# Moving adaLN accumulations, expert loads, key transposes and one shift vector within the hand-written order of an attention stage

## The chip, the cores and the metric

The kernel runs on one core of a Trainium2 chip. The metric is the device time of one execution in microseconds (us), median of three runs. TensorE (PE) multiplies and transposes, VectorE (DVE) and ScalarE (ACT) work on the results, GpSimd (POOL) takes some elementwise work, and SyncE (SP) issues nearly all transfers from the chip's memory, one after another in its own program order.

## The reference, cut to what matters

One layer of a diffusion transformer over 256 latent tokens `x` and 256 context tokens, width 1024, in float32:

```
mod = split(silu(c) @ w_ada + b_ada, 6)              # six vectors of 1024
h   = modulate(rms_norm(x), mod[0], mod[1])           # context tokens likewise, with c_ctx
y   = token_mixing(h, hc, ...)                        # 8 heads windowed GQA with sinks, 8 heads MLA, @ w_o
x   = x + mod[2] * rms_norm(y)
h2  = modulate(rms_norm(x), mod[3], mod[4])
f   = moe_ffn(h2, ...)                                # router, top 4 of 32 experts, clamped SwiGLU
x   = x + mod[5] * rms_norm(f)
```

The weights of the 32 experts are 32 x 12 MB. Every expert is computed, for the tokens that chose it, so all 384 MB are read in each execution.

## The kernel before, in words

The program has three stages: projections (to about 117 us), attention (to about 237 us) and experts (to the end).

**Attention.** The 16 heads are worked in 8 units of two heads, u = 0 to 3 for GQA and u = 4 to 7 for MLA. For each unit `weights(u)` computes the transposed logits on PE into PSUM tiles (named `mm`, four buffers shared by nearly everything in this stage) and takes their exponential on ACT; `adds(u)` sums them on POOL; `values(u)` multiplies by the values on PE and divides on DVE; `mix(u)` multiplies the unit's output by its part of `w_o` and adds into the four tiles `y`. A softmax needs a shift, the largest logit of a row: `top_a` and `top_b` compute it (PE, then a DVE reduce into `mx`), and `shift(g)` turns the sign on DVE, transposes on PE (L649) and copies to `nmax` on ACT (L651), which `weights` then adds by a matmul with `sel`. `shift("a")` serves units 0 to 3, `shift(0)` units 4 and 5, `shift(1)` units 6 and 7. For MLA the keys of four token blocks are prepared by `k_mid(i)` (two ACT copies, L529 and L530, the first of which reads the projection `pk[i]` out of PSUM) and `k_flip(i)` (eight PE transposes, L536, into two `tp` buffers; ACT casts, L137, with a DVE partner).

**Ada pieces.** Of the six adaLN vectors, four are accumulated along the way: index `ch` 0 (`mod[2]`, tile `accw_105`, called `vmix`), 1 (`mod[3]`, `accw_106`), 2 (`mod[4]`, `accw_107`), 3 (`mod[5]`, `vpost`). Each takes four loads of 1 MB of `w_ada`, so there are 16 pieces. `ada_load()` issues the DMA of the next piece (L418) into a tile of the three-buffer ring `slot`, or of a small pool `ax`; `ada_do()` takes the oldest loaded piece and adds it with two DVE instructions of 128x1024 (L431, called a pair here). `ada(1)` in the attention stage is a load of the next piece and the pair of an older one. When a vector's four pieces are in, `column(1)`, `column(2)`, `spread1(0)` and `spread1(3)` use it: a column is eight small matmuls and DVE work, `spread1` is two halves, each two PE instructions in the trace (L604) and one DVE product (L605). `router_bias()` needs `column(1)`.

**Expert loads.** `load(e, js)` issues 1 MB pieces of the expert weights, each into the next of 18 buffers in the order `RSEQ`; the three-buffer ring `slot` is among them, so an expert load there waits until the ada piece before it in that buffer has been consumed. The first three go out in the middle of attention, the others from `load(0, range(3, 6))` on. In the expert stage L1021 is the matmul with an expert's weights, and a later load waits until PE has finished with the buffer's former content.

**Order.** From L749 on the order on every engine, SP's queue included, is the order in which the code calls these functions; nothing is rearranged. Semaphores between engines are set from the data and the buffers. The calls are the list that starts with the two `ada_load()` behind `manual_schedule` and ends with `mix(KD - 1)`.

Of the kernel before, what the change touches and what calls it, by code (L numbers as in the profile page):

```python
# [70 lines left out]
def layer_kernel(ctx, tc, x, cx, cc, wadr, bada, grows, win0, winB, winC, winD, wuqa, wuqb, wukv, wo, wr, wexp, bgu, bgx, bdn, cols, rows, consts, out):  # L71
# [335 lines left out]
    ada_n = [0]  # L407
    ada_q = []
# [12 lines left out]
    def ada_do(n=1):  # L421
        for _ in range(n):
            ch, s, w = ada_q.pop(0)
            a = accs[ch]
            for k in range(2):
                sk = silu[:, 2 * s + k, 0:1]
                if (ch, s, k) in ADA_G:
                    S.activation(w[:, k], w[:, k], AF.Copy, scale=sk)
                    G.tensor_tensor(a, a, w[:, k], op=ALU.add)
                else:  # L430
                    V.scalar_tensor_tensor(a, w[:, k], sk, a, op0=ALU.mult, op1=ALU.add)  # L431
# [10 lines left out]
    def top_a(j, t):  # L442

        s_ = [pmm((P, 512)) for h in range(2)]
        kb = 3 - t
        for h in range(2):
            PE.matmul(s_[h][:, kb * P:(kb + 1) * P], ident_b, mask_b[:, t * P:(t + 1) * P], start=True, stop=False,
                      skip_group_check=True)
        for h in range(2):
            PE.matmul(s_[h], qTg[0][HALF[h], t, j], kTg[0][HALF[h]], start=False, stop=True, skip_group_check=True)  # L450
        for h in range(2):
            V.tensor_reduce(mxs["a"][:, t, 64 * h + j:64 * h + j + 1], s_[h], axis=AX.X, op=ALU.max)
# [35 lines left out]
    def up(i, p_, ws):  # L488
        for k in range(2):
            mm3(p_, (ckvT[0][:, i, k], ckvT[1][:, i, k]), ws[k], k == 0, k == 1)  # L490
        return p_

    for t in range(NT):
        top_a(3, t)
    ada_do()
    pk = {i: up(i, prow() if i < 2 else pmm(), ws) for i in (2, 3, 0, 1)}
    st1.close()
# [29 lines left out]
    def k_mid(i):  # L527
        k96[i] = pqa.tile([P, 8, 96], F32, name="k96", tag="ct", bufs=2)
        S.copy(k96[i][:, :, 0:64], pk[i].rearrange("p (h d) -> p h d", h=8))  # L529
        S.copy(k96[i][:, :, 64:96], krt[:, i][:, None].to_broadcast([P, 8, 32]))  # L530

    def k_flip(i):
        for g in range(2):
            pt = ptp((96, 4, P))
            for j in range(4):
                PE.transpose(pt[:, j], k96[i][:, g * 4 + j], ident)  # L536
            ks = slice(i * P, (i + 1) * P)
            split(kTm[0][g][0:96, :, ks], kTm[1][g][0:96, :, ks], pt)
# [57 lines left out]
        S.dma_start(gs_[ch], bass.AP(tensor=grows.tensor, offset=grows.offset + (0 if ch == 0 else 1) * D,  # L596
                                             ap=[[0, P], [1, D]]))

    def spread1(ch):
        a, gs = accs[ch], gs_[ch]  # L600
        for n in range(2):
            sl = slice(n * 512, (n + 1) * 512)
            p_ = pmm((P, 512))
            PE.matmul(p_, ones_f, a[:, sl], start=True, stop=True)  # L604
            V.tensor_tensor(a[:, sl], p_, gs[:, sl], op=ALU.mult)  # L605
# [25 lines left out]
    def top_b(h):  # L631
        n, j = divmod(h, 4)
        for t in range(NT):
            s_ = pmm((P, 512))
            PE.matmul(s_, qTm[n][0:96, 0, t, j], kTm[0][n][0:96, j], start=True, stop=True)
            V.tensor_reduce(mxs[n][:, t, j:j + 1], s_, axis=AX.X, op=ALU.max)

    def shift(g):

        m = mxs[g]  # L640
        if g == "a":
            m4 = m.rearrange("p t (h c) -> p t h c", h=2)[:, :, :, 0:4]
            V.scalar_tensor_tensor(m4, m4, -1.0, nsink.rearrange("p (h j) -> p h j", h=2)[:, None].to_broadcast([P, NT, 2, 4]),
                                   op0=ALU.mult, op1=ALU.min)
        else:
            V.tensor_scalar(m[:, :, 0:4], m[:, :, 0:4], -1.0, None, op0=ALU.mult)
        p_ = pmm((P, T))
        for t in range(NT):
            PE.transpose(p_[:, t * P:(t + 1) * P], m[:, t], ident)  # L649
        r = rows_[g] = av.tile([P, T], F32R, name="nmax", tag="nmax", bufs=2)  # L650
        S.copy(r, p_)  # L651
        if g == "a":
            for h in range(2):
                ess[h] = av.tile([P, T], F32, name=f"es{h}")
                S.activation(ess[h], r.bitcast(F32), AF.Exp, scale=A_SCALE, bias=col[:, G_SINK + h:G_SINK + h + 1])
# [4 lines left out]
    def weights(u):  # L660

        a = u < 4
        pT_[u] = [av.tile([P, 4, T], F32, name="pT", bufs=4) for h in range(2)]
        for g in range(2):
            st = [pmm((P, 2, T)) for h in range(2)]
            for kk in range(2):
                kt = 2 * g + kk
                ks = slice(kt * P, (kt + 1) * P)
                ops = []
                for h in range(2):  # L670
                    if a:
                        k_ = [x_[HALF[h], ks] for x_ in kTg]
                        q_ = [x_[HALF[h], :, u] for x_ in qTg]
                        sl, r = sel[HALF[h], u], rows_["a"][HALF[h]]
                    else:
                        n, j = divmod(2 * (u - 4) + h, 4)
                        k_ = [x_[n][0:96, j, ks] for x_ in kTm]
                        q_ = [qTm[n][0:96, i, :, j] for i in range(2)]
                        sl, r = sel[0:96, j], rows_[n][0:96]
                    ops.append([(k_[0], q_[0]), (k_[0], q_[1]), (k_[1], q_[0]), (sl, r)])  # L680
                for i in range(4):
                    for h in range(2):
                        PE.matmul(st[h][:, kk], *ops[h][i], start=(kk == 0 and i == 0), stop=(i == 3 and not (a and g)),  # L683
                                  skip_group_check=True)
                if a and g:
                    t = 3 - kt
                    for c in range(2):
                        for h in range(2):
                            PE.matmul(st[h][:, kk, t * P + c * 64:t * P + c * 64 + 64], mask_s[HALF[h], t, c],
                                      ident_b[HALF[h], HALF[h]], start=False, stop=True, skip_group_check=True)  # L690
            for h in range(2):
                S.activation(pT_[u][h][:, 2 * g:2 * g + 2], st[h], AF.Exp, scale=A_SCALE if a else B_SCALE)  # L692
        adds(u)
# [58 lines left out]
    ada_load()  # L752
    v_split()
    k_mid(2)
    k_mid(3)
    shift("a")
    weights(0)
    k_flip(2)
    k_mid(0)
    weights(1)  # L760
    k_flip(3)
    k_mid(1)
# [37 lines left out]
    shift(0)  # L800
    top_b(4)
    top_b(5)
    mix(2)
    column(1)
    weights(4)
    ada(1)
    top_b(6)
    top_b(7)
    mix(3)
    load_wo(3)  # L810
    ada(1)
    router_bias()
    spread1(0)
    shift(1)
    weights(5)
    ada(1)
# [2 lines left out]
    weights(6)  # L819
    mix(4)  # L820
    ada(1)
    column(2)
    values(5)
    spread0(3)
    ada(1)
    load(0, range(3, 6))
    weights(7)
    mix(5)
    ada(1)
    values(6)  # L830
    load(0, range(6, 8))
    load(1, range(0, 1))
    ada(1)
    mix(6)
    assert ada_n[0] == 16 and not ada_q
    values(7)
    spread1(3)
    mix(KD - 1)
    st2.close()
    stB.close()  # L840
# [515 lines left out]
```

## Time and profile before

| what | value |
|---|---|
| runs | 1195.87, 1200.46, 1198.42 us; median 1198.42 us |
| profiled execution | 1200.95 us, span of its trace 1199.2 us |
| PE busy | 1106.7 us, 92% of the span |
| DVE, ACT, POOL busy | 304.8, 231.4, 129.2 us |
| mean granted clock of TensorE | 0.980 |
| data moved | 446.58 MB, 372 GB/s over the span |

The span is the time from the first to the last instruction of the profiled execution; its run time is 1.75 us longer. The granted clock is told as a share of full speed: 1.00 is 2.4 GHz, 0.50 is 1.2 GHz. In the rows below, a mark such as [2.17 <-ACT nmax L651] behind an instruction says that its engine was idle for 2.17 us ahead of it and that this ended with ACT's writing of `nmax` at line 651. A row of a timeline may hold several instructions of one kind (x4); its second number is the time from the first one's start to the last one's end.

### The profile page before, as it was taken

The page shows a single profiled execution, that of the slowest core. Times are in us where ns is not written, and L with a number is a line of the kernel's source. Part 1 is how long each engine was busy: PE and PEld are TensorE (multiplying, and loading weights), DVE is VectorE, ACT ScalarE, POOL GpSimd, SP SyncE. Part 2 cuts the span into 40 slices and gives each one's busy share as a digit, 9 for nine tenths or more (in the row PEclk, how much of TensorE's full clock was granted, in tenths as well). Part 3 has the DMA queues.
Part 4 walks back from the last instruction along what each step waited for, and adds up shares of the span by engine and source line. Part 5 has one row for each costly group of instructions (what it writes and reads, how often), then busy time and mean ns, then how long its engine had stood idle before and what let it go on. Part 6 is the DMA issues. An engine that isn't in the chain of part 4 may idle for free.

```text
span 1199.2 us, 13600 instructions
## 1 busy us (share of the span) xinstructions
PE 1106.7 (92%) x5441; PEld 475.2 (40%) x5441; DVE 304.8 (25%) x651; ACT 231.4 (19%) x509; POOL 129.2 (11%) x186
## 2 busy tenths in 40 slices
PE   7699999999999999999989999999899999999985
PEld 2587757553343434333333333333333333333321
DVE  3776566742111111111111111111111111111112
ACT  3533612121111111111111111111111111111101
POOL 0301413210101010100101010101010101010000
PEclk9889999998999999999999999999999999999998
DMA  9740093899999999999999999999999999999994
GB/s 379 300 163 22 36 365 140 325 409 421 403 420 420 421 419 420 420 419 421 421 420 421 421 419 421 421 421 419 420 421 421 420 421 421 420 420 421 420 421 166
DMA packets 63194, 446.58 MB, mean 372 GB/s; under 512 B 7284, under 2 KB 7540, under 8 KB 10008
## 3 DMA queue, kind: packets, MB, share of 16 engines
q1 hardware_dynamic: 62648, 444.24, 89.9%
q10 hardware_dynamic: 480, 1.44, 0.3%
q8 instruction: 44, 0.72, 0.2%
q14 instruction: 22, 0.18, 0.0%
HBM read 444.60 MB, written 1.05 MB: 372 GB/s over the span
## 4 chain that ended last, share of the span: by engine, by line
DMA 64%; PE 29%; DVE 4%; issue 1%; ACT 1%; POOL 0%; SPq 0%; POOLq 0%; ACTq 0%; DVEq 0%
DMA slot<-in_wexp 63%; PE pw L1021 11%; PE y L723 2%; PE mm L683 2%; PE mm L274 2%; PE px L988 1%; PE mm L707 1%; PE mm L148 1%; PE mm L146 1%; PE mm L147 1%; PE acc L1051 1%; PE pr L547 1%; DVE accw L431 1%; DVE rz L717 1%; PE pf L1034 1%
## 5 line engine op out<-in xcount | busy, mean ns | idle before, releaser
L1021 PE MATMUL pw<-slot,xg 128*64 128x512 f32 x2048 | 468.2, 599 | 19.1 <-DMA slot<-in_wexp 19.1
L1021 PE MATMUL pw<-slot,actT 128*64 128x512 f32 x1024 | 242.8, 601 | 29.7 <-DMA slot<-in_wexp 28.1
L1021 PEld LDWEIGHTS pw<-slot,xg 128*64 128x64 f32 x2048 | 136.5, 136 | 302.5 <-issue 234.2
L1039 DVE TENSOR_TENSOR z<-pf,bg 128x512 f32<-128x512 f32 x64 | 44.3, 692 | 756.4 <-PE pf L1034 756.4
L1021 PEld LDWEIGHTS pw<-slot,actT 128*64 128x64 f32 x1024 | 68.6, 136 | 180.1 <-issue 101.0
L1043 ACT ACTIVATE sg<-z 128x256 f32<-128x256 f32 x64 | 26.7, 417 | 312.8 <-DVE z L1041 312.8
L1028 ACT COPY gu<-pw 128x512 f32<-128x512 f32 x64 | 37.5, 585 | 230.4 <-PE pw L1021 230.4
L988 PEld LDWEIGHTS px<-oh,xt 128*128 128x128 f32 x480 | 57.5, 196 | 23.9 <-issue 23.9
L1051 PE MATMUL acc<-y,ctt 64*128 64x512 f32 x256 | 63.6, 615 | 0.7 <-ACT y L1028 0.7
L988 PE MATMUL px<-oh,xt 128*128 128x128 f32 x480 | 63.3, 287 | 0.3 <-DVE cnt L1106 0.3
L1000 ACT ACTIVATE xg<-px,vcol 128x128 f32<-128x128 f32 x120 | 45.1, 456 | 92.0 <-PE px L988 92.0
L1034 PEld LDWEIGHTS pf<-con,gu 128*128 128x128 f32 x256 | 26.8, 140 | 52.7 <-issue 51.1
L1034 PE MATMUL pf<-con,gu 128*128 128x128 f32 x256 | 42.0, 287 | 0.7 <-ACT gu L1028 0.7
L1028 ACT COPY y<-pw 128x512 f32<-128x512 f32 x32 | 18.7, 585 | 91.7 <-PE pw L1021 91.7
L723 PE MATMUL y<-slot,of 128*128 128x512 f32 x64 | 31.9, 642 | 2.5 <-DVE of L718 2.3
L978 POOL TENSOR_SCALAR oh<-con,posm,r 128x64 f32<-128x64 f32 x60 | 33.8, 580 | 2.5 <-DVE posm L918 2.5
L1045 DVE TENSOR_TENSOR sg<-z,sg 128x256 f32<-128x256 f32 x64 | 27.2, 425 | 18.1 <-ACT sg L1043 18.1
L1051 PEld LDWEIGHTS acc<-y,ctt 64*128 64x128 f32 x256 | 22.1, 186 | 21.8 <-issue 18.4
L698 POOL TENSOR_TENSOR pa<-pT 128x512 f32<-128x512 f32 x16 | 21.6, 1347 | 68.1 <-ACT pT L692 57.2
L1046 DVE SCALAR_TENSOR_TENSOR actT<-z,sg 128x256 f32<-128x256 f32 x64 | 27.2, 425 | 2.2
L274 PE MATMUL mm<-slot,siluz 128*4 128x512 f32 x40 | 19.3, 633 | 7.4 <-DMA slot<-in_wadr 7.4
L124 POOL TENSOR_TENSOR rstd<-rstd,mh 128x1 f32<-128x1 f32 x14 | 10.3, 733 | 137.7 <-DVE rstd L121 133.8
(449 smaller groups left out, 870.5 us busy)
## 6 DMA issues: line engine op xcount, KB each, us to landing
slot<-in_wexp SPq DMA_DIRECT2D x384, 1024.0 KB, 19.8
slot<-in_wadr SPq DMA_DIRECT2D x20, 1024.0 KB, 8.7
ax<-in_wadr SPq DMA_DIRECT2D x4, 1024.0 KB, 6.1
slot<-in_wo SPq DMA_DIRECT2D x4, 1024.0 KB, 4.9
slot<-in_win SPq DMA_DIRECT2D x2, 1024.0 KB, 10.0
slot<-in_winD SPq DMA_DIRECT2D x2, 768.0 KB, 9.9
slot<-in_winB SPq DMA_DIRECT2D x2, 576.0 KB, 5.6
ct<-in_cx SPq DMA_DIRECT2D x2, 512.0 KB, 8.5
```

What stands on the lines that cost most here:

```text
L274: PE.matmul(pad[ch][n], siluz[:, 2 * s + k], w[:, k, n * 512:(n + 1) * 512], start=(s == 0 and k == 0), stop=(last and k == 1), skip_group ...
L723: PE.matmul(y[t][n], oT[k][:, t * P:(t + 1) * P], wov[k][:, n * 512:(n + 1) * 512], start=(k == 0), stop=(k == KD - 1), skip_group_check=True)
L978: eng.tensor_scalar(oh[t][:, i], iota[:, 0:CAP], pos_ap(t), r2[t], op0=ALU.is_equal, op1=ALU.mult)
L988: PE.matmul(px[:, k, 0:ne * CAP], xt[t][:, kk * P:(kk + 1) * P], self.oh[t][:, 0:ne].rearrange("p e c -> p (e c)"), start=(k == 0 and t == ...
L1000: S.activation(o, i, AF.Identity, scale=vcol[:, 1, kk:kk + 1], bias=vcol[:, 0, kk:kk + 1])
L1021: PE.matmul(pt[HALF[h]], lhs(k), wk(k, h), start=(k == 0), stop=(k == KD - 1), skip_group_check=True)
L1028: S.copy(y, pt)
L1034: PE.transpose(pf[:, b].rearrange("p h c -> p (h c)"), gu[:, b * P:(b + 1) * P], ident)
L1039: V.tensor_tensor(z, pf, bias[:, :, :, None].to_broadcast([P, 4, 2, CAP]), op=ALU.add)
L1045: V.tensor_tensor(sg, zg, sg, op=ALU.mult)
L1046: V.scalar_tensor_tensor(actT[:, 4 * c:4 * c + 4], zl, 1.0, sg, op0=ALU.add, op1=ALU.mult)
L1051: PE.matmul(acc[t][n], ctt[HALF[n], t], y[HALF[n]], start=False, stop=last, skip_group_check=True)
```

## The change

One more ada piece is loaded and added during the projections, ahead of and behind `top_a(3)`, and in attention the later pieces stand earlier in the list: one `ada(1)` ahead of `weights(0)`, one behind `k_mid(0)`, and none behind `column(2)`, where three stood. The loads of the experts, whose place in the list is unchanged, then have fewer ada loads ahead of them in SP's queue. `shift("a")` stands ahead of `k_mid(3)`, and `k_flip(2)` ahead of `weights(0)`. `column(1)` stands ahead of `mix(2)`. One `ada(1)` that stood ahead of `router_bias()` now stands behind `spread1(0)`, directly ahead of `shift(1)`. `spread1(3)` is split into its halves, one ahead of `mix(6)` and one ahead of `mix(7)`. The lines of the changed file from 495 on carry numbers that are two or more higher. The diff, without some lines of context:

```diff
@@ -490,8 +490,10 @@
+    ada_load()
     for t in range(NT):
         top_a(3, t)
+    ada_do()
     ada_do()
@@ -596,9 +598,9 @@
-    def spread1(ch):
+    def spread1(ch, ns=(0, 1)):
         a, gs = accs[ch], gs_[ch]
-        for n in range(2):
+        for n in ns:
@@ -752,11 +754,13 @@
     ada_load()
     v_split()
     k_mid(2)
+    shift("a")
     k_mid(3)
-    shift("a")
+    k_flip(2)
+    ada(1)
     weights(0)
-    k_flip(2)
     k_mid(0)
+    ada(1)
     weights(1)
     k_flip(3)
     k_mid(1)
@@ -800,17 +804,17 @@
     shift(0)
     top_b(4)
     top_b(5)
+    column(1)
     mix(2)
-    column(1)
+    ada(1)
     weights(4)
-    ada(1)
     top_b(6)
     top_b(7)
     mix(3)
     load_wo(3)
-    ada(1)
     router_bias()
     spread1(0)
+    ada(1)
     shift(1)
     weights(5)
     ada(1)
@@ -819,22 +823,20 @@
     weights(6)
     mix(4)
     ada(1)
+    assert ada_n[0] == 16 and not ada_q
     column(2)
     values(5)
     spread0(3)
-    ada(1)
     load(0, range(3, 6))
     weights(7)
     mix(5)
-    ada(1)
     values(6)
     load(0, range(6, 8))
     load(1, range(0, 1))
-    ada(1)
+    spread1(3, (0,))
     mix(6)
-    assert ada_n[0] == 16 and not ada_q
     values(7)
-    spread1(3)
+    spread1(3, (1,))
     mix(KD - 1)
```

**ScalarE at the start of attention.** In the order of before, from the key copies of `k_mid(2)` to the casts of the first key transposes, ACT has:

```order
L529 COPY k_1058<-mm 128x8x64
L530 COPY k_1058<-krt 128x8x32
L529 COPY k_1061<-mm 128x8x64
L530 COPY k_1061<-krt 128x8x32
L373 ACTIVATE cqT<-tp,col 128x128 x3
L512 CAST sel<-con 64x512 x2
L651 CAST nmax<-mm 128x256
L655 ACTIVATE es_1070<-nmax,col 128x256
L655 ACTIVATE es_1072<-nmax,col 128x256
L692 ACTIVATE pT<-mm 128x512 x4
L137 CAST kTm_1022<-tp 96x4x128
L137 CAST kTm_1023<-tp 96x4x128
```

The same place in the changed order, where `k_1075` is the tile of `k_mid(3)`, is:

```order
L531 COPY k_1062<-mm 128x8x64
L532 COPY k_1062<-krt 128x8x32
L373 ACTIVATE cqT<-tp,col 128x128 x3
L514 CAST sel<-con 64x512 x2
L653 CAST nmax<-mm 128x256
L657 ACTIVATE es_1071<-nmax,col 128x256
L657 ACTIVATE es_1073<-nmax,col 128x256
L531 COPY k_1075<-mm 128x8x64
L532 COPY k_1075<-krt 128x8x32
L137 CAST kTm_1028<-tp 96x4x128
L137 CAST kTm_1029<-tp 96x4x128
L694 ACTIVATE pT<-mm 128x512 x4
```

The two copies of `k_mid(3)` moved from ahead of `nmax` to behind `es`, and the two casts of the key transposes from behind the four exponentials of unit 0 to ahead of them.

**VectorE around `shift(1)`.** In the order of before DVE has, from the last reduce of `top_b(7)` on:

```order
L636 TENSOR_REDUCE mx<-mm 128x1 x4
L431 SCALAR_TENSOR_TENSOR accw_107<-slot,silu,accw_107 128x1024 x2
L626 TENSOR_TENSOR rb<-mm,row 128x32
L605 TENSOR_TENSOR accw_105<-mm,gs 128x512 x2
L646 TENSOR_SCALAR mx<-mx 128x2x4
L431 SCALAR_TENSOR_TENSOR accw_107<-slot,silu,accw_107 128x1024 x2
```

In the changed order the same place is:

```order
L638 TENSOR_REDUCE mx<-mm 128x1 x4
L628 TENSOR_TENSOR rb<-mm,row 128x32
L607 TENSOR_TENSOR accw_105<-mm,gs 128x512 x2
L431 SCALAR_TENSOR_TENSOR vpost<-slot,silu,vpost 128x1024 x2
L648 TENSOR_SCALAR mx<-mx 128x2x4
L431 SCALAR_TENSOR_TENSOR vpost<-slot,silu,vpost 128x1024 x2
```

The pair of 128x1024 instructions moved from ahead of `rb` (`router_bias`) and the two products of `spread1(0)` to between them and the sign change of `shift(1)`.

**SyncE's queue at the last ada loads.** In the order of before SP issues, from the last-but-one load of `w_o` on:

```order
L582 DMA slot<-in_wo 128x2048
L418 DMA slot<-in_wadr 128x2048
L582 DMA slot<-in_wo 128x2048
L418 DMA slot<-in_wadr 128x2048
L415 DMA vpost<-in_bada 1x1024
L418 DMA slot<-in_wadr 128x2048 x4
L740 DMA slot<-in_wexp 128x2048 x3
```

In the changed order, from that load of `w_o` on, it issues:

```order
L584 DMA slot<-in_wo 128x2048
L418 DMA slot<-in_wadr 128x2048
L584 DMA slot<-in_wo 128x2048
L418 DMA slot<-in_wadr 128x2048 x2
L742 DMA slot<-in_wexp 128x2048 x3
```

Three ada loads, whose `slot` buffers the expert loads take over, have gone from between the last load of `w_o` and the fourth to sixth expert load.

## Rows read from the trace of the kernel before

**Rows 1.** The page's chain that ended last, by line.

```profile
DMA slot<-in_wexp 63%; PE pw L1021 11%; PE y L723 2%; PE mm L683 2%; PE mm L274 2%; PE px L988 1%; PE mm L707 1%; PE mm L148 1%; PE mm L146 1%; PE mm L147 1%; PE acc L1051 1%; PE pr L547 1%; DVE accw L431 1%; DVE rz L717 1%; PE pf L1034 1%
```

**Rows 2.** Expert windows: length, busy PE, PEld, DVE, ACT, POOL; PEclk, DMA share, GB/s.

```profile
380.00:1180.00 800.00, 750.88 (x3544) 270.59 (x3541) 112.07 (x275) 118.77 (x268) 57.77 (x101) 1.00 1.01 419
...
296.00:306.00 10.00, 10.00 (x52) 4.68 (x52) 0.00 (x0) 3.01 (x8) 0.00 (x0) 0.94 1.01 419
306.00:314.00 8.00, 8.00 (x40) 2.77 (x38) 1.62 (x4) 1.00 (x2) 0.00 (x0) 1.00 0.93 348
```

**Rows 3.** Expert load issued in 216:217, in 254.6:255.2, in 306.2:306.8; last column landing.

```profile
slot<-in_wexp SPq DMA_DIRECT2D x1, 1024.0 KB, 4.7
...
slot<-in_wexp SPq DMA_DIRECT2D x1, 1024.0 KB, 12.1
...
slot<-in_wexp SPq DMA_DIRECT2D x1, 1024.0 KB, 5.4
```

**Rows 4.** What SP's queue waited for, 120 to 320 us: total, times, longest.

```profile
SPq L740 <- PE pw L1021: 36.5, 20, 5.4
```

**Rows 5.** Timeline of PE at the start of attention: start, length, instruction, idle before.

```profile
117.66 0.49 PE L369 MATMUL tp<-con,cn 128*128 128x128 f32 x3
...
120.86 0.39 PE L683 MATMUL mm<-nmax,sel 64*128 64x256 f32 x2 [2.17 <-ACT nmax L651]
...
122.83 1.08 PE L536 MATMUL tp<-con,k 128*96 128x128 f32 x8
```

**Rows 6.** Timeline of ACT at the start of attention.

```profile
117.64 0.58 ACT L529 COPY k<-mm 128x512 f32<-128x512 f32 x1 [0.50 <-PE mm L148]
...
118.43 0.89 ACT L373 ACTIVATE cqT<-tp,col 128x128 f32<-128x128 f32 x3
...
120.44 0.37 ACT L651 CAST nmax<-mm 128x256 fp32r<-128x256 f32 x1
...
121.76 2.26 ACT L692 ACTIVATE pT<-mm 128x512 f32<-128x512 f32 x4
123.91 1.07 ACT L137 CAST kTm<-tp 96x512 fp32r<-96x512 f32 x2
```

**Rows 7.** Timeline of DVE around column(1) and shift(1).

```profile
173.99 2.48 DVE L636 TENSOR_REDUCE mx<-mm 128x1 f32<-128x512 f32 x4 [0.84 <-PE mm L635]
...
187.82 3.96 DVE L431 SCALAR_TENSOR_TENSOR accw<-slot,silu,accw 128x1024 f32<-128x1024 f32 x2
...
191.81 1.27 DVE L605 TENSOR_TENSOR accw<-mm,gs 128x512 f32<-128x512 f32 x2
193.00 0.15 DVE L646 TENSOR_SCALAR mx<-mx 128x8 f32<-128x8 f32 x1
193.07 2.59 DVE L431 SCALAR_TENSOR_TENSOR accw<-slot,silu,accw 128x1024 f32<-128x1024 f32 x2
```

**Rows 8.** Timeline of PE at shift(1).

```profile
190.07 1.96 PE L604 MATMUL mm<-accw,con 128*128 128x512 f32 x4
193.30 0.41 PE L649 MATMUL mm<-con,mx 128*128 128x128 f32 x2 [1.27 <-DVE mx L646]
```

**Rows 9.** Timeline of PE from mix(6) to mix(7).

```profile
224.24 5.40 PE L723 MATMUL y<-slot,of 128*128 128x512 f32 x8 [2.34 <-DVE of L718]
...
231.88 1.98 PE L604 MATMUL mm<-vpost,con 128*128 128x512 f32 x4
233.70 3.60 PE L723 MATMUL y<-slot,of 128*128 128x512 f32 x8
```

**Rows 10.** Timeline of DVE, unit 7's division, first half.

```profile
233.01 0.29 DVE L718 TENSOR_TENSOR of<-mm,rz 128x128 f32<-128x128 f32 x1
```

**Rows 11.** Windows of attention, for the granted clock (PEclk).

```profile
121.40:124.80 3.40, 3.40 (x54) 3.08 (x52) 0.28 (x1) 3.30 (x7) 1.19 (x1) 1.00 0.00 0
...
222.00:225.40 3.40, 1.16 (x3) 0.68 (x4) 3.34 (x3) 0.00 (x0) 1.98 (x2) 1.00 0.64 270
225.50:228.90 3.40, 3.40 (x5) 1.33 (x4) 1.20 (x1) 0.00 (x0) 0.00 (x0) 0.50 0.27 53
```

## Prediction

> **What bounds the kernel now.** I read the page's chain first, then windows of the expert stage with the landings of expert loads, and last the timelines of PE, ACT and DVE where the change moves something. In the chain the reader sees that transfers of expert weights end last for 63% of the span, and that work on PE comes next [rows 1]. The windows say where the one hands over to the other. From 380 to 1180 us the transfers run at 419 GB/s with the DMA engines full, so a 1 MB load takes 1,048,576 B / 419 GB/s = 2.50 us, and nothing that PE does there counts [rows 2]. From 296 to 306 us the rate is as high, but PE is busy for all of the 10 us, and from 306 to 314 us, with PE busy throughout, the rate falls to 348 GB/s [rows 2]. The load issued at 306.3 us lands after 5.4 us; a load that finds the transfers idle, as the one at 216.5 us, lands after 4.7 us [rows 3]. So the queue was almost empty at 306 us, and SP was waiting there for PE to hand back buffers: 20 waits on L1021 in 120 to 320 us [rows 4]. The time of PE's work up to about 306 us therefore starts the full stream that sets the end, and the question is what the change does to PE's path through attention, plus the little that earlier loads can still add.
>
> **The sum's base.** The durations come from the profiled execution, 1200.95 us, which is 2.53 us over the median of 1198.42 us. I add the terms to 1200.95 and then take 2.53 off.
>
> **Projections.** One more pair of DVE instructions (2.59 us for such a pair, rows 7) and one load. They lie beside PE's projection matmuls, which need neither. I take 0, with 2.59 us as the upper end if that cover is gone and 0 as the lower, since nothing is removed there.
>
> **Start of attention.** The wait to be filled is 2.17 us, and it ends with ACT's `nmax` [rows 5]. On ACT the two copies of `k_mid(3)`, 118.43 − 117.64 = 0.79 us, leave the place ahead of `nmax` [rows 6]; but the copies of `cqT`, next in the order, read transposes that PE ends at 117.66 + 0.49 = 118.15 us [rows 5], so they start only 118.43 − 118.15 = 0.28 us sooner, and `nmax` at 120.16 instead of 120.44 us [rows 6]. From `nmax` to the exponentials are 121.76 − 120.44 = 1.32 us [rows 6], so ACT is through with `es` at 121.48 us. There it now has the 0.79 us of `k_mid(3)` and the 1.07 us of casts, and the exponentials of unit 0 start at 123.34 us instead of 121.76 us, 1.58 us later [rows 6].
> On PE the eight transposes of `k_flip(2)`, 1.08 us, leave their old place at 122.83 us and run in the wait [rows 5]. With the 0.28 us PE could be 1.36 us ahead. Two things take that back. The second half of `weights(0)` needs the `mm` buffer that `pk[3]` holds until `k_mid(3)`'s first copy ends at 121.48 + 0.58 = 122.06 us, which costs about 0.8 us. And `weights(1)`, now directly behind `weights(0)`, needs buffers that the exponentials empty: one exponential is 2.26 / 4 = 0.57 us [rows 6], so the first two are free at 123.9 and 124.5 us, while before `weights(1)` began where the transposes ended, at about 123.9 us. Its two heads alternate, so PE is held by something between 0 and 0.6 us: I take +0.4 us. The ends are −1.36 us (nothing waits for ACT) and +1.58 us (all of ACT's delay passes on).
>
> **column(1).** Ahead of `mix(2)` its matmuls need a `mm` buffer, which a reduce of `top_b` must first empty; a reduce is 2.48 / 4 = 0.62 us [rows 7]. Between 0 and 0.62 us I take +0.2 us.
>
> **shift(1).** Before, the pair ahead of `rb` runs at 187.82 us, beside PE's `mix(3)` and spread matmuls; it takes 3.96 us there, and PE waits 1.27 us for the sign change [rows 7, 8]. Now DVE comes to `rb` at once, and the products wait for PE's spread matmuls, which end at 190.07 + 1.96 = 192.03 us [rows 8]. The last product, 1.27 / 2 = 0.64 us [rows 7], ends at about 192.7 us. Then stands the pair, 2.59 us, ahead of the sign change at 195.3 us. PE's transposes followed the sign change's start by 193.30 − 193.00 = 0.30 us [rows 7, 8], so they come at 195.6 instead of 193.30 us: +2.3 us. Behind them on PE stand all of `weights(5)` and what follows, so nothing else fills the wait, now 195.6 − 192.03 = 3.6 us. Lower end +2.0 us (the pair runs 0.3 us faster than its row), upper end +3.7 us (the pair takes 3.96 us here).
>
> **spread1(3).** The wait ahead of `mix(6)` is 2.34 us [rows 9]; half of the spread, 1.98 / 2 = 0.99 us, fits into it. At `mix(7)` PE could then begin 0.99 us sooner than at 233.70 us [rows 9], but the first half of `of` is ready at 233.01 + 0.29 = 233.30 us [rows 10], so the gain is 0.4 us. Ends −0.99 and 0 us: −0.4 us.
>
> **The granted clock.** After the wait ahead of `mix(6)` PE is busy for 3.40 us at 0.50 (1.2 GHz instead of 2.4), having been busy for 1.16 us of the 3.40 us before; after the wait of 2.17 us it stays at 1.00 [rows 11]. A stretch at 0.50 does half its length of work, so it costs 3.40 / 2 = 1.7 us. The change shortens the idle time ahead of `mix(6)` to 2.34 − 0.99 = 1.35 us, which may save that fall, and makes a longer one, 3.6 us, at `shift(1)`, which may bring one. I set the two against each other: 0, with ends −1.7 and +3.4 us (two stretches).
> The Trainium skill, TensorE: Matmul & The Clock Gate, section "Part 1: The HAM clock gate", says that the throttled state is the default, that activity lifts it, and that the moment of the change is not the same in every run. By this rule the longer wait at `shift(1)` speaks against the change: one stretch more would make the sum 1.7 us larger, 1202.1 us. The trace agrees as far as it goes: of two waits over 2 us one was followed by 0.50 and the other was not [rows 11].
>
> **Earlier expert loads.** Three ada loads leave the queue ahead of the fourth expert load. The load at 254.6 us lands after 12.1 us, so 12.1 − 4.7 = 7.4 us of transfers lie ahead of it, and these will have been done sooner [rows 3]. At 306.3 us only 5.4 − 4.7 = 0.7 us of that is left [rows 3], and the shortfall of the window to 314 us is 8 x (1 − 348 / 419) = 1.36 us [rows 2]. So I take −0.5 us, between 0 and −1.4 us.
> The Trainium skill, DMA: Bandwidth & Descriptors, section "Rules for kernel authors", advises to issue a DMA early and to wait for it late, so that its cost lies beside compute. Taken alone that would make the advance count to the end, which is the first rival below; here the waits on PE [rows 4] bear it out only as far as buffers are free.
>
> **Sum.** 0 + 0.4 + 0.2 + 2.3 − 0.4 + 0 − 0.5 = +2.0 us; 1200.95 + 2.0 − 2.53 = 1200.4 us.
>
> **Rivals.**
> *The loads' advance is carried to the end.* If the stream from 254 us on is bound by transfers alone, the end moves by the 7.4 us: 1200.95 − 7.4 − 2.53 = 1191.0 us, or 1193.5 us with PE's 2.5 us (the sum without its last term) against it. For it speaks the full rate from 296 to 306 us, against it the lag of 5.4 us at 306 us and the fall to 348 GB/s behind it. Chance 0.16.
> *The waits are filled as meant.* The transposes and the 0.28 us (−1.36), the half spread in full (−0.99), no fall of the clock ahead of `mix(7)` (−1.7) and −0.5 from the loads, and the pair ahead of `shift(1)` done before the products, which would take a PE that comes to them later: −4.55 us, 1193.9 us. Against it: the order puts the pair behind the products and the casts ahead of the exponentials. Chance 0.14.
> *The clock falls at shift(1).* The wait of 3.6 us brings two stretches at 0.50 (+3.4) and the fall ahead of `mix(7)` stays: 0.4 + 0.2 + 2.3 − 0.4 + 3.4 = +5.9 us without a gain from the loads, 1204.3 us, and 1205.5 us if ACT's whole delay at the start passes on (1.58 for 0.4). It decides if the clock is at 0.50 for two such stretches, 6.8 us, behind 196 us. For it speaks that a shorter wait, 2.34 us, was enough for one stretch, against it that PE then has `weights(5)` and the matmuls of `values(4)` to do without a DVE step between them, where the clock can come back after one. Chance 0.22.
> My forecast has 0.48, with its own range of 1197 to 1204 us.
>
> **From cases to numbers.** Within 0.5% of the median (about what a measurement of this kernel can tell from no change) is 1192.4 to 1204.4 us. Of the first rival half lies below (0.08), of the second, together with some of the first's advance, half (0.07): faster 0.15. Of the third two thirds lie above (0.14), and 0.01 of my forecast: slower 0.15. The rest, 0.70, is no change. The range from 1192.5 to 1206.0 us leaves out most of the first rival's lower end and the third's upper end, together under 0.2.
>
> **What would show it.** Right: in the changed trace PE waits some 3.6 us ahead of `shift(1)`'s transposes and the releaser is DVE's sign change; the exponentials of unit 0 start about 1.6 us later against `nmax`; the wait ahead of `mix(6)` holds half a spread; expert loads land up to 7 us sooner at 255 us and within 1 us of PE's shift at 306 us, and the rate behind that is again 419 GB/s. Wrong: a time below 1196 us with the loads at 306 us ahead by more than 3 us, or PE's path shorter at `mix(7)` than before.

## The result, and the profile after

The changed kernel takes 1205.84 us (median of five runs, 1204.01 to 1208.44), the kernel before 1198.95 us (median of five, 1195.87 to 1202.35). The ratio is 1.0063, with an interval of 1.0045 to 1.0080: slower by some 7 us, where 1200.4 us and no change were forecast.

The profiled execution of the changed kernel is the fastest of its five (1204.01 us, span 1202.2 us), that of before lay 2.53 us over its median. Their spans therefore differ by 3.0 us only, and their mean granted clocks by 0.003 (0.980 before, 0.983 after), so the trace of before holds more time at 0.50. What of the 7 us these two traces don't show has to come from runs of single edits. First the places where they do differ. A timeline of PE in the changed kernel, from `shift("a")` to the transposes behind `values(0)` (columns as in [rows 5]; L651 is the shift's transpose, L538 `k_flip`, L685 `weights`, L709 and L711 `values`):

```profile
116.84 0.38 PE L651 MATMUL mm<-con,mxa 128*128 128x128 f32 x2
...
120.03 0.39 PE L685 MATMUL mm<-nmax,sel 64*128 64x256 f32 x2 [0.31 <-ACT nmax L653]
...
121.43 0.62 PE L685 MATMUL mm<-slot,slot 64*128 64x256 f32 x5 [0.43 <-ACT k L531]
...
123.20 1.10 PE L685 MATMUL mm<-slot,slot 64*128 64x256 f32 x6 [0.32 <-ACT pT L694]
...
131.43 0.43 PE L711 MATMUL mm<-pa,con 128*64 128x256 f32 x1 [2.03 <-POOL pa L701]
...
132.44 0.75 PE L538 MATMUL tp<-con,k 128*96 128x128 f32 x5
```

The same two ends in the kernel before:

```profile
117.44 0.38 PE L649 MATMUL mm<-con,mxa 128*128 128x128 f32 x2
...
129.92 1.08 PE L536 MATMUL tp<-con,k 128*96 128x128 f32 x8
```

The wait of 2.17 us for `nmax` [rows 5] is down to 0.31 us, as the change means it to be. But from the shift's transposes to those behind `values(0)` PE took 129.92 − 117.44 = 12.48 us before and takes 132.44 − 116.84 = 15.60 us now: 3.1 us more. Most of it is the new wait of 2.03 us for POOL's `pa`, the sums of unit 0's exponentials. POOL's timeline after shows them:

```profile
124.19 1.64 POOL L700 TENSOR_TENSOR pa<-pT 128x512 f32<-128x512 f32 x1 [6.81 <-ACT pT L694]
125.91 1.59 POOL L701 TENSOR_TENSOR pa<-pa 128x256 f32<-128x256 f32 x1
127.46 2.24 POOL L700 TENSOR_TENSOR pa<-pT 128x512 f32<-128x512 f32 x1
129.78 1.59 POOL L701 TENSOR_TENSOR pa<-pa 128x256 f32<-128x256 f32 x1
```

and before:

```profile
123.61 1.29 POOL L698 TENSOR_TENSOR pa<-pT 128x512 f32<-128x512 f32 x1 [5.63 <-ACT pT L692]
124.98 0.74 POOL L699 TENSOR_TENSOR pa<-pa 128x256 f32<-128x256 f32 x1
125.68 1.27 POOL L698 TENSOR_TENSOR pa<-pT 128x512 f32<-128x512 f32 x1
127.03 0.73 POOL L699 TENSOR_TENSOR pa<-pa 128x256 f32<-128x256 f32 x1
```

The same four instructions take 7.06 us instead of 4.03 us. What runs beside them now is on DVE, two ada pairs in a row:

```profile
123.41 7.38 DVE L431 SCALAR_TENSOR_TENSOR accw<-slot,silu,accw 128x1024 f32<-128x1024 f32 x4
```

At `shift(1)` the changed kernel's DVE and PE (rows of two timelines, against [rows 7, 8]):

```profile
194.36 2.59 DVE L431 SCALAR_TENSOR_TENSOR vpost<-slot,silu,vpost 128x1024 f32<-128x1024 f32 x2
196.87 0.17 DVE L648 TENSOR_SCALAR mx<-mx 128x8 f32<-128x8 f32 x1
...
191.75 1.96 PE L606 MATMUL mm<-accw,con 128*128 128x512 f32 x4
197.18 0.41 PE L651 MATMUL mm<-con,mx 128*128 128x128 f32 x2 [3.47 <-DVE mx L648]
```

and from `mix(6)` to `mix(7)` (against [rows 9]):

```profile
227.22 1.12 PE L606 MATMUL mm<-vpost,con 128*128 128x512 f32 x2
229.63 3.70 PE L725 MATMUL y<-slot,of 128*128 128x512 f32 x8 [1.29 <-DVE of L720]
233.26 1.95 PE L709 MATMUL mm<-pT,vm 128*64 128x256 f32 x16
...
237.05 1.13 PE L725 MATMUL y<-slot,of 128*128 128x512 f32 x2 [0.35 <-DVE of L720]
```

Windows of the changed kernel for the granted clock and for the expert stage (columns as in [rows 2]):

```profile
194.40:197.80 3.40, 0.62 (x6) 0.65 (x7) 3.37 (x5) 0.17 (x1) 0.00 (x0) 1.00 1.01 429
197.90:201.30 3.40, 3.40 (x18) 3.40 (x17) 1.66 (x2) 0.83 (x3) 0.00 (x0) 0.50 1.00 386
...
229.60:233.00 3.40, 3.37 (x8) 1.44 (x8) 0.57 (x1) 0.00 (x0) 0.00 (x0) 1.00 1.02 424
...
299.50:309.50 10.00, 10.00 (x53) 4.91 (x54) 0.00 (x0) 3.01 (x8) 0.00 (x0) 0.96 0.55 220
309.50:317.50 8.00, 8.00 (x40) 2.77 (x38) 1.61 (x4) 1.00 (x2) 0.00 (x0) 1.00 0.82 288
...
380.00:1180.00 800.00, 751.32 (x3544) 270.97 (x3546) 110.53 (x271) 119.23 (x269) 60.95 (x106) 1.00 1.01 420
```

The clock falls behind the longer wait at `shift(1)` and no longer behind the one ahead of `mix(6)`. A third stretch differs: during `weights(4)` the clock was at 0.50 before, though PE was busy for all of the 3.4 us ahead of it, and is at 1.00 now (the first row is before, the second after).

```profile
181.10:184.50 3.40, 3.40 (x19) 3.40 (x18) 2.43 (x2) 1.08 (x2) 0.00 (x0) 0.50 0.00 0
182.50:186.00 3.50, 3.50 (x29) 3.26 (x28) 0.80 (x1) 1.08 (x2) 0.00 (x0) 1.00 0.09 37
```

The expert loads are further ahead than PE can use: from 299.5 to 309.5 us, where before 419 GB/s were moved [rows 2], it is 220 GB/s with PE busy for all 10 us. The transfers stand idle for part of that time, and start their full stream when PE hands back buffers.

### The profile page after: what moved, and what is told of

Read it like the earlier page. It is cut to its first block, busy times and chain, and to the rows that moved or that the text cites. A ratio compares the mean times of both kernels' runs of the same rounds, so it can differ in the third digit from the quotient of the medians.

```text
span 1202.2 us, 13597 instructions
## 1 busy us (share of the span) xinstructions
PE 1106.9 (92%) x5441; PEld 474.4 (39%) x5441; DVE 304.1 (25%) x651; ACT 231.0 (19%) x509; POOL 128.9 (11%) x186
## 3 DMA queue, kind: packets, MB, share of 16 engines
HBM read 444.60 MB, written 1.05 MB: 371 GB/s over the span
## 4 chain that ended last, share of the span: by engine, by line
DMA 56%; PE 36%; DVE 4%; ACT 1%; issue 1%; POOL 1%; SPq 0%; POOLq 0%; ACTq 0%; DVEq 0%
DMA slot<-in_wexp 55%; PE pw L1023 17%; PE y L725 2%; PE px L990 2%; PE mm L274 2%; PE acc L1053 2%; PE mm L685 1%; DMA slot<-in_wadr 1%; PE mm L709 1%; PE mm L148 1%; PE mm L146 1%; PE mm L147 1%; PE pf L1036 1%; DVE rz L719 1%; PE pr L549 1%
## 5 line engine op out<-in xcount | busy, mean ns | idle before, releaser
L1017 ACT COPY ctt<-px 128x256 f32<-128x256 f32 x32 | 12.0, 375 | 62.0 <-PE px L1016 62.0
```

## The experiments

Theory A, formed on these rows: two steps cost the time. The early ada pairs slow POOL's adds of unit 0, for which PE then waits (2.5 to 3 us), and the pair ahead of the sign change keeps PE waiting at `shift(1)` (2.2 us, more with a stretch at 0.50); the earlier loads are worth nothing. Rival B: the transfers that were brought forward cost the time. Rival C: low-clock stretches alone make the difference. Every ratio below is to the kernel before on the same chip, with its 95% interval; the changed kernel's is 1.0063.

**The early ada pieces moved back (first try).**

```diff
     k_flip(2)
-    ada(1)
     weights(0)
     k_mid(0)
-    ada(1)
     weights(1)
...
     v_up(1)
+    ada(1)
     q_up(1, 0)
...
     v_up(2)
+    ada(1)
     q_flip(1, 0)
```

> The changed kernel with its two early ada pieces (ahead of weights(0) and behind k_mid(0)) moved behind v_up(1) and v_up(2). Theory A: in the changed kernel these four DVE accumulations run at 123.4 to 130.8 us beside POOL's adds of unit 0, which took 2.24 and 1.59 us where before they took 1.27 and 0.73 us, and PE waited 2.03 us for the last of them; moved away, POOL is back at 1.3 and 0.7 us, PE's wait for pa at values(0) is under 0.5 us, and the time falls by 2.5 to 3 us from 1205.8, to about 1203. Rival B (the transfers that were brought forward cost the time, by colliding with others): no gain, 1205 to 1207. Rival C (the difference is low-clock stretches that follow any wait): PE's wait goes, but the time only falls if a stretch at 0.50 goes with it.

Measured: 1.0114 (1.0100 to 1.0129), slower than the changed kernel. POOL's adds are back at 1.29, 0.74, 1.28 and 0.73 us and no wait for `pa` is left, but PE waits elsewhere, as its timeline shows:

```profile
156.85 0.71 PE L637 MATMUL mm<-kTm,qTm 96*128 96x512 f32 x2
165.80 1.19 PE L725 MATMUL y<-slot,of 128*128 128x512 f32 x1 [8.24 <-DMA slot<-in_wo]
```

`ada(1)` is also a load, and each load in SP's queue waits for a `slot` buffer that an ada pair must empty. The two loads of `w_o` stand behind them, were issued at 157.1 us (in the changed kernel from 152.98 us on) and landed after 9.6 us (7.6 us). So the time says nothing of theory A; its trace does. An ada piece that moves takes SP's queue along.

**`shift(1)` ahead of the ada piece.**

```diff
     spread1(0)
-    ada(1)
     shift(1)
+    ada(1)
```

> The changed kernel with shift(1) ahead of the ada piece that stands between it and spread1(0). Theory A: the sign change no longer waits for a pair of 2.59 us, PE's wait at shift(1) falls from 3.47 us to about 1.2 us, and the stretch at 0.50 behind it (197.9 to 201.3 us) goes in most runs: 2.2 us, with the stretch 3.9 us, so 1202 to 1203.6. Rival B: no gain, 1205 to 1207. Rival C: about 1.7 us, only by the stretch.

Measured: 1202.29 us, 1.0035 (1.0022 to 1.0048): about 0.28%, 3.4 us, less than the changed kernel. PE's wait and the windows around it in this kernel:

```profile
196.49 0.41 PE L651 MATMUL mm<-con,mx 128*128 128x128 f32 x2 [0.95 <-DVE mx L648]
```

```profile
193.00:196.40 3.40, 2.54 (x8) 0.98 (x6) 1.71 (x5) 0.00 (x0) 0.33 (x1) 1.00 0.47 147
196.50:203.00 6.50, 6.50 (x55) 5.40 (x55) 4.88 (x4) 2.54 (x5) 1.64 (x2) 1.00 1.00 396
```

The wait is 2.5 us shorter and the clock stays at 1.00. This is as theory A has it; rival B gives no gain and is out for this part. The interval just overlaps that of the changed kernel (1.0045 to 1.0080), so the size of the gain is loose.

**Both of these edits.**

> Both of these edits in the changed kernel. Theory A: 5 to 6.6 us less than the changed kernel, 1199.2 to 1201, within 2 us of the kernel before although its expert loads are issued as early as in the changed one, so that their advance is worth nothing by itself. Rival B: 1205 to 1207. A gain of the earlier loads, if there were one: below 1196.

Measured: 1.0105 (1.0080 to 1.0131). The wait for `w_o` of the first try is in it too (8.19 us), so it decides nothing.

**Two ada pieces early, in the kernel before.**

```diff
     shift("a")
+    ada(1)
     weights(0)
     k_flip(2)
     k_mid(0)
+    ada(1)
     weights(1)
...
     v_up(0)
-    ada(1)
     weights(2)
...
     q_up(1, 0)
-    ada(1)
     weights(3)
```

> The kernel before with nothing changed but two ada pieces of attention, from behind v_up(0) and q_up(1, 0) to ahead of weights(0) and behind k_mid(0), where the changed kernel has them. Theory A: POOL's adds of unit 0 slow to 1.6 to 2.2 us, PE waits about 2 us for them at values(0), and the time is 2 to 3 us over the kernel before's 1199. Rival B and rival C without a stretch at 0.50: as the kernel before, within 1 us.

Measured: 0.9996 (0.9987 to 1.0005), no change; theory A's number failed. The trace shows why. In this order the first pair's first instruction runs at 117.04 us, before there is anything to add on POOL, and only one pair's time (3.49 us for two instructions) lies beside the adds. POOL's second add is slowed to 2.46 us, but the exponentials are as early as before, and PE waits only 0.32 us for it. So the slowing alone does not cost the 2 us. In the changed kernel the exponentials come later as well: the two pairs start 0.8 us ahead of POOL's first add, and all four of its instructions are slowed. The run does not price the slowing by itself: a wait of 1.05 us at `shift(0)` is new in it, and the mean granted clock of its eleven runs is 0.985 against 0.983 of the kernel before.

**The early ada pieces moved back (second try).**

```diff
     values(0)
     k_flip(0)
+    ada(1)
     q_up(0, 0)
...
     k_flip(1)
+    ada(1)
     q_up(0, 1)
```

with the two early ones taken out as in the first try.

> The changed kernel with its two early ada pieces moved again, but to behind k_flip(0) and k_flip(1), so that the ada loads ahead of w_o in SP's queue find their buffers in time (moved further back, they held w_o up until PE waited 8.24 us for it at mix(0)). Theory A (POOL's adds of unit 0 beside the two pairs): POOL at 1.3 and 0.7 us, no wait for pa at values(0), no wait for w_o, 2.5 to 3 us under the changed kernel's 1205.8, so about 1203. Rival B (the early transfers cost the time): 1205 to 1207. Rival C (low-clock stretches): no gain beyond one stretch, 1.7 us.

Measured: 1204.70 us, 1.0041 (1.0024 to 1.0058): 0.22%, 2.6 us, less than the changed kernel, with intervals that overlap, so by itself the time does not show the gain. The trace does. PE's timeline (its `shift("a")` transposes are at 117.27 us):

```profile
127.45 1.95 PE L709 MATMUL mm<-pT,vg 128*64 128x256 f32 x16
129.23 0.60 PE L711 MATMUL mm<-pa,con 128*64 128x256 f32 x4
129.66 0.60 PE L714 MATMUL mm<-es,sel 128*64 128x256 f32 x4
130.19 1.08 PE L538 MATMUL tp<-con,k 128*96 128x128 f32 x8
```

No wait is left at `values(0)`, and PE needs 130.19 − 117.27 = 12.92 us for the piece that took 15.60 us with the pairs: 2.7 us are the pairs'. What remains over the 12.48 us of before, 0.44 us, is the order of ACT and of the key transposes. The exponentials are as late as in the changed kernel: POOL's first add comes 7.35 us after the shift's transposes in both (124.62 − 117.27 and 124.19 − 116.84). So their lateness alone makes no wait for `pa`. A new wait of 1.24 us at `q_up` takes part of the gain.

**The same, and `shift(1)` ahead of the ada piece.**

> The same, and shift(1) ahead of the ada piece, which by itself gave 1202.3. Theory A: the two gains add up, 1202.3 - 2.7 = 1199.6, between 1198.5 and 1200.5, with the expert loads as early as in the changed kernel. Rival B: 1202 to 1204. If the loads' advance were worth something: under 1196.

Measured: 1200.84 us against 1201.21 us of the kernel before on that chip, 1.0004 (0.9987 to 1.0020). With the two steps undone, the whole of the 0.63% is gone. The early pairs' part shows here too: against the run with `shift(1)` alone ahead (1.0022 to 1.0048) it is 0.31%, 3.7 us, with intervals that do not overlap, though on another chip. All the rest of the change (earlier expert loads, key transposes in the wait, `column(1)`, the split spread), together with new waits of 1.24 us at `q_up` and 1.05 us at `shift(0)` that the moved pairs bring, is worth nothing that can be measured; its parts were not tried one by one. Rival B falls for the expert loads: the fourth is issued at 200.79 us, in the changed kernel at 199.62 us, before at 216.53 us. It falls for the early ada loads by the changed kernel's own trace: from 123.4 to 127 us, where the adds and the pairs are slowed, the transfers move 2 GB/s, while at `shift(1)` the pair takes its usual 2.59 us beside 429 GB/s. Rival C falls as the whole account: the gain of the second try is a wait of PE, not a stretch at 0.50 (both traces have two of these in attention), though a stretch has its part at `shift(1)`.

**Both pairs beside the adds, in the kernel before.**

```diff
     weights(0)
     k_flip(2)
+    ada(1)
     k_mid(0)
+    ada(1)
     weights(1)
```

with the pieces behind `v_up(0)` and `q_up(1, 0)` taken out.

> The kernel before with two ada pieces moved to directly behind k_flip(2) and k_mid(0), so that both pairs stand on DVE behind the key casts and run from about 125 us beside POOL's adds of unit 0. Nothing else is moved; ACT's order is that of before. Theory A: POOL's second add of unit 0 takes 2.2 to 2.5 us instead of 1.27, PE waits 1 to 2 us at values(0), and unit 0's division on DVE waits for the pairs: 1 to 2.5 us over the kernel before, 1199.6 to 1201. Rival D (the wait at values(0) comes from ACT's later exponentials alone): no wait for pa, as the kernel before within 0.6 us.

Measured: 1206.08 us, 1.0046 (1.0031 to 1.0061), 5 us over the kernel before and more than expected. DVE and POOL in its trace, and PE behind them:

```profile
127.06 7.36 DVE L431 SCALAR_TENSOR_TENSOR accw<-slot,silu,accw 128x1024 f32<-128x1024 f32 x4
134.35 1.27 DVE L138 TENSOR_TENSOR kTl<-tp,kTm 96x512 fp32r<-96x512 f32 x2
```

```profile
127.01 2.46 POOL L698 TENSOR_TENSOR pa<-pT 128x512 f32<-128x512 f32 x1
129.55 1.60 POOL L699 TENSOR_TENSOR pa<-pa 128x256 f32<-128x256 f32 x1
131.11 2.24 POOL L698 TENSOR_TENSOR pa<-pT 128x512 f32<-128x512 f32 x1
```

```profile
131.20 0.43 PE L709 MATMUL mm<-pa,con 128*64 128x256 f32 x1 [0.31 <-POOL pa L699]
...
135.08 1.94 PE L536 MATMUL tp<-con,k 128*96 128x128 f32 x8 [2.80 <-DVE kTl L138]
```

The four DVE instructions take 7.36 us, as in the changed kernel (7.38 us), and POOL's add and its second step 2.46 and 1.60 us (there 2.24 and 1.59 us). Rival D's number, no change, fails; that late exponentials alone make no wait, the second try showed. But theory A's wait for `pa` is not met either, 0.31 us where 1 to 2 us were expected: here PE waits for DVE rather than for POOL. The casts of `k_flip(3)` stand behind the two slowed pairs, and `k_flip(0)` needs their `tp` buffers. From the shift's transposes to `k_flip(0)` PE takes 135.08 − 118.78 = 16.30 us, 3.8 us more than before, and behind the wait the granted clock is 0.52 from 135.0 to 138.4 us, which adds to it. Slow pairs hurt twice, through POOL and through what stands behind them on DVE. In the changed kernel those casts came at 130.71 us, hidden behind the wait for `pa`.

**The kernel before without its last three ada pieces.**

```diff
     spread0(3)
-    ada(1)
     load(0, range(3, 6))
     weights(7)
     mix(5)
-    ada(1)
...
-    ada(1)
     mix(6)
```

> The kernel before without its last three ada pieces: the last load of w_ada and three DVE pairs are left out, so that vpost holds only the first quarter of its sum. PE's order is that of before. The fourth and later expert loads are issued 6 to 13 us sooner, as in the changed kernel. Theory A (PE hands back the buffers from about 255 us on, and the advance is spent there): the load near 306 us is issued at the same time within 0.5 us, and the time is that of the kernel before within 1.5 us. Rival (the advance is carried to the end): 6 to 7 us faster, 1191 to 1193.

Measured: 0.9989 (0.9970 to 1.0007). A gain of 6 to 7 us, 0.994 to 0.995, is excluded. The load at `254.6` us of [rows 3] has its counterpart at 253.71 us and lands after 5.2 us instead of 12.1 us, so 7 us more of the transfers are done; the one at 306.32 us has its counterpart at 305.26 us, 1.06 us sooner, and as much (1.07 us) PE is ahead in this execution already at `shift("a")`, 116.37 against 117.44 us. The windows say where the 7 us go (columns as in [rows 2]):

```profile
295.00:305.00 10.00, 10.00 (x51) 4.60 (x52) 0.00 (x0) 3.01 (x8) 0.00 (x0) 0.94 0.67 238
305.00:313.00 8.00, 8.00 (x40) 2.77 (x38) 1.66 (x5) 1.00 (x2) 0.00 (x0) 1.00 0.84 312
```

PE is busy throughout, and the transfers, 238 GB/s instead of 419, wait for its buffers.

**The ada piece ahead of `shift(1)`, in the kernel before.**

```diff
-    ada(1)
     router_bias()
     spread1(0)
+    ada(1)
     shift(1)
```

> The kernel before with one edit: the ada piece ahead of router_bias() moved to between spread1(0) and shift(1), where the changed kernel has it. Theory A: PE's wait at shift(1) grows from 1.27 to about 3.5 us, 2.2 us, and with a stretch at 0.50 behind it 3.9 us: 1.0018 to 1.0033 of the kernel before. Rival (the loss at shift(1) exists only together with the earlier loads): no change.

Measured: 1.0037 (1.0022 to 1.0051), a little over what was expected. PE's wait is 3.47 us, to the hundredth that of the changed kernel, and in the profiled execution two stretches at 0.50 follow it:

```profile
194.10:201.00 6.90, 6.18 (x29) 6.21 (x30) 3.10 (x4) 1.46 (x3) 0.00 (x0) 0.51 0.28 118
```

The step costs the time without any earlier load, by its wait (2.2 us) and by the clock that it brings down: the mean granted clock of its twelve runs is 0.980, that of the 35 runs of the kernel before on the chip 0.983. The clock does not fall as often in each run: they lie between 1199.43 us at 0.983 and 1206.90 us at 0.977.

**`sel` made on POOL, in the kernel before.**

```diff
-        S.copy(sel[hp], ident[...
+        G.tensor_copy(sel[hp], ident[...
```

> The kernel before with the two casts that make sel (1.24 us on ACT ahead of nmax) put on POOL, which is idle there. Theory: the wait of 2.17 us at weights(0) is ACT's, so it falls to about 0.9 us and the time by up to 1.2 us, 0.999 of the kernel before. Rival: PE then waits for the exponentials' buffers instead and nothing is gained.

Measured: 0.9990 (0.9980 to 0.9999). PE's wait for `nmax` is 1.03 us instead of 2.17 us; the gain is just clear of none. The wait that the change set out to fill could be halved at its source.

**No pair ahead of a step that PE waits for.** From the second try with `shift(1)` ahead:

```diff
-    ada(1)
     q_up(0, 1)
     values(1)
+    ada(1)
...
     top_b(3)
-    ada(1)
     mix(1)
...
-    column(1)
     mix(2)
     ada(1)
+    column(1)
     weights(4)
+    ada(1)
...
     load_wo(3)
+    shift(1)
     router_bias()
     spread1(0)
-    shift(1)
     ada(1)
```

> The changed kernel with the ada pieces moved so that no pair stands ahead of a step that PE waits for: the early two behind k_flip(0) and values(1), one from ahead of shift(0) to behind mix(2), and shift(1) ahead of router_bias() and spread1(0). Theory: against the version with only the first two of these moves (1.0004 of the kernel before) the waits of 1.05, 0.95 and 1.24 us go, 3 us: 0.998 of the kernel before. Rival: new waits for mm buffers behind the reduces take 1 to 2 us of it.

Measured: 0.9989 (0.9977 to 1.0001). The waits at both shifts and at `q_up` are gone from the trace, and one of 0.74 us at a `weights` is new. Against the version it starts from that is 0.15%, 1.8 us, where 3 us were expected; the two intervals overlap, and so does this one with no change.

**The same, with the start of before and `sel` on POOL.**

> The last version with the start of attention in the order of the kernel before (both k_mid ahead of the shift, k_flip(2) behind weights(0)) and sel made on POOL. Theory: about 1.5 us less again, 0.996 to 0.997 of the kernel before, faster than both kernels. Rival: as the version without it.

Measured: 1196.38 us against 1198.88 us, 0.9975 (0.9963 to 0.9987), faster than both kernels, a little less than expected. Against the last version (0.9977 to 1.0001) the intervals overlap. PE's waits of 0.7 us and more in attention add up to 5.1 us in its trace, the longest 1.51 us and none at a shift.

## Why the prediction was wrong, point by point

**What bounds the kernel: right.** PE's path to about 306 us sets the end. In the changed kernel the load with the place of the one at 306.32 us was issued at 309.82 us, 3.5 us later, and the span grew by 3.0 us; the forecast had 0.5 us as the loads' share. The experiment without the last ada pieces shows the advance spent.

**Projections: right as far as traces tell.** `shift("a")`'s transposes start between 116.37 and 118.78 us in the six traces without the additional piece and between 116.41 and 117.70 us in the eight with it.

**Start of attention: the step that failed.** It was put at +0.4 us, at most +1.58 us, from ACT's order, the key transposes and the buffers of `mm`. That part measured +0.44 us (the second try: 12.92 against 12.48 us), and the exponentials came 122.54 − 119.60 = 2.94 us behind `nmax` instead of 1.32 us, 1.6 us later as forecast. What the step left out are the two ada pairs that the change puts on DVE there. They were counted nowhere, neither as DVE work nor for what they hold up, because the working goes by the order of ACT and PE at this place and not by that of DVE and POOL. They cost 2.7 us on PE in the trace; in the runs the two comparisons give 2.6 us, not clear of the noise, and 3.7 us, clear of it, both with the new wait of 1.24 us against the gain. The hint stood in [rows 7]: the pair at 187.82 us took 3.96 us and the one at 193.07 us 2.59 us, and I took the one as an upper bound without asking what made it slow. It was POOL's adds, which run at 187.78 and 189.12 us.
The Trainium skill, SBUF — State Buffer, section "Who interferes with whom", says that a DVE instruction with two SBUF inputs contends with a GpSimd instruction that reads SBUF, and not with one that only writes it, and that the shared port pair behind this is "an exclusive lock". The trace agrees. The pair has two SBUF inputs and POOL's adds read SBUF. A POOL memset, which only writes, lay beside a pair at 202.18 us of the kernel before: it took 0.95 us, as elsewhere, and the pair 2.62 us. And the four DVE instructions of the changed kernel, taken one by one, wait for POOL's in turn:

```profile
123.41 1.27 DVE L431 SCALAR_TENSOR_TENSOR accw<-slot,silu,accw 128x1024 f32<-128x1024 f32 x1
124.71 2.20 DVE L431 SCALAR_TENSOR_TENSOR accw<-slot,silu,accw 128x1024 f32<-128x1024 f32 x1
126.95 1.63 DVE L431 SCALAR_TENSOR_TENSOR accw<-slot,silu,accw 128x1024 f32<-128x1024 f32 x1
128.61 2.17 DVE L431 SCALAR_TENSOR_TENSOR accw<-slot,silu,accw 128x1024 f32<-128x1024 f32 x1
```

The first runs in its usual 1.27 us, to 124.68 us. From then on the two engines end by turns, POOL at 125.83, DVE at 126.91, POOL at 127.50, DVE at 128.58 us and so on. Each instruction ends 0.59 us (POOL's 128x256) or 1.08 to 1.15 us (the others) after the other engine's, which is its time alone (0.73 and 1.27 us) less 0.1 to 0.2 us. So the work was done nearly one after another, and most of what is added to a duration is waiting for the other engine.

**shift(1): right in its wait, short in what follows.** Forecast were +2.3 us and a wait of 3.6 us; PE came 197.18 − 191.75 = 5.43 us after the start of the spread matmuls instead of 3.23 us, +2.2 us, with a wait of 3.47 us.

**The granted clock: the mechanism as forecast, the balance open.** The term was 0, with a new fall at `shift(1)` set against one saved ahead of `mix(6)`. Both happened in the profiled execution, +1.5 us and −1.7 us, and they are no accident of it. All four traces here with a wait of 3.47 us at `shift(1)` have 0.50 behind it (one stretch in three of them, two in the fourth), and none of the eight with a wait of 0.95 to 1.27 us there. Behind the 2.34 us ahead of `mix(6)` five of six traces have a stretch, and none of the eight with the half spread in it and 1.29 us left. By these counts the new fall costs somewhat more than the saved one. Over the runs, moving `shift(1)` ahead gave 3.4 us where the wait is 2.5 us shorter, and the same piece put into the kernel before cost 0.37%, 4.4 us, for a wait that is 2.2 us longer. The third stretch, at 181.10 us before, stood in no term; PE's lag behind the kernel before shrinks there from 182.46 − 179.59 = 2.87 us to 191.75 − 190.07 = 1.68 us, and other traces of either order have it or not. The third rival has the fall at `shift(1)` right, but it kept the fall ahead of `mix(7)`, which is gone, and lacks the 2.7 us: that its time, 1204.3 to 1205.5 us, came near the result is luck.

**spread1(3) and column(1): right.** −0.4 us forecast; `mix(7)` began 237.05 − 233.26 = 3.79 us after `values(7)` instead of 233.70 − 229.57 = 4.13 us, −0.34 us, and the wait is for `of`, as worked out. `column(1)` cost nothing that shows: from `shift(0)` to `weights(4)` PE takes 182.46 − 176.07 = 6.39 us instead of 179.59 − 173.27 = 6.32 us.

**The base.** The sum was set against a profiled execution 2.53 us over its median. One difference is seen at 39.9 us, far from the change: in the trace of before the instruction of POOL below takes 3.00 us, in that of the changed kernel 0.99 us, and PE waits 2.09 us at 52.31 us in the one and 0.70 us at 50.64 us in the other. By `shift("a")` 0.60 us of the lead is left (116.84 against 117.44 us).

```profile
39.90 3.00 POOL L124 TENSOR_TENSOR rstd<-rstd,mh 128x1 f32<-128x1 f32 x1 [0.16 <-DVE rstd L121]
```

**What is left.** The forecast was +2.0 us, and measured were some 7 us (5.4 to 9.6 us by the interval). Of the 5 us between them 2.7 us are the pairs'. The counts of stretches give the clock some 0.7 us more (an estimate: 5 stretches in 4 traces less 5 in 6, at 1.5 to 1.7 us each), which brings the sum to the lower end of the interval. The rest, between nothing and some 4 us, is open; part of it can be how the clock fell in the runs that have no trace.

The first rival (the advance carried to the end) is refuted by the experiment without the last ada pieces, the second (waits filled as meant) by the timeline: the wait for `nmax` was filled, and one for `pa` took its place.

## What to carry to other kernels

When work moves, list every engine it runs on, and look at what runs beside it there and on the engines that share its inputs; two instructions whose durations are known alone may not keep them together. A step in front of which an engine waits should have nothing ahead of it on its own queue that could stand behind it: here moving the pairs by that rule took the waits at both shifts away; the fastest kernel here also has `sel` on POOL and the start of before. Transfers that are issued sooner gain nothing while the buffers behind them come back at the consumer's pace.

## What the runs showed of the hardware

DVE's 128x1024 accumulation and POOL's 128x512 add, both with two inputs in SBUF, hardly run beside each other but take turns: two pairs beside the adds took 7.36 to 7.39 us in three traces where 4 x 1.30 us are usual, and an add 2.24 to 2.46 us instead of 1.27 us. DVE's casts `kTl<-tp,kTm`, one input of which is in PSUM, and POOL's adds do not hold each other up: at 124.52 us of the kernel before the two casts take 1.28 us, and the adds beside them 0.74 and 1.27 us.

A wait of 3.47 us on PE brought one stretch at 0.50 in three traces and two in a fourth; waits of 0.95 to 1.27 us at the same place brought none in eight. A wait of 2.34 us brought one in five traces of six. The times of one kernel follow the clock: of 34 runs of the kernel before on one chip, the 22 with a mean granted clock of 0.980 took 1202.0 us on average, the six with 0.986 took 1196.3 us.
